# Output projections in products of 128 columns, four sums side by side in one PSUM bank

## The chip, the cores and the metric

The kernel runs on one core of one Trainium2 chip. The core has a matrix engine (TensorE, in the profile PE for matmuls and PEld for the loads of the stationary operand), a vector engine (DVE), a scalar engine (ACT), a general engine (POOL, or GpSimd) and a queue that issues most transfers (SP). Matmuls write into PSUM, eight banks of 2 KiB for each of 128 partitions; 512 float32 numbers fill one bank. The metric is the device time of one execution in microseconds (us).

## What is computed

One inference step of a decoder with two layers, for a prompt of 2048 tokens and for a sample batch of 8 sequences with 4 new tokens each (32 rows). Every layer normalises, projects in, mixes, projects out and adds the residual. The part that the change touches is the product with `w_out` at the end of either layer:

```python
def even_mixer(h, w_in, b_fox, lb, hgrn_gain, w_out, hgrn_s0, fox_attend):
...
    out = jnp.concatenate([o_a, o_b], axis=-1) @ w_out
    return out, s_a, kb_h, vb_h, log_fb

def odd_mixer(h, w_in, w_gate, b_gate, gla_gain, w_out, gla_s0):
...
    o = head_rmsnorm(o, gla_gain).reshape(bsz, L, C_VAL_WIDTH).astype(h.dtype) * jax.nn.silu(g)
    return o @ w_out, s

def run_trunk(...):
...
        x = x + out
    return rmsnorm(x, final_norm), ...
```

Here `w_out` is 1024 x 1024. The even layer has two groups of heads (a gated linear recurrence, and forgetting attention, which for the sample batch reads a paged cache of keys and values); the odd layer has one group, a gated linear recurrence.

## The kernel before

**Precision.** A float32 operand is held as two float16 parts, high and low, after scaling by a power of two. Every product is three matmuls into one sum: high by high, high by low, low by high (`mm3`, L476). Its three lines, L478 to L480, therefore stand for nearly all dense matmuls of the kernel, and groups of the profile are told apart by their tiles.

**Halves and units.** The 2048 prompt tokens are worked in two halves of 1024; the first half also carries the 32 sample rows. A half of a layer is a list of units, each with 256 (for one 272 or 260) columns of a weight. A unit has four stages: fetch the weights by DMA, measure their largest value, turn it into a scale, split into high and low parts (`half_unit`, L315; the split goes in four parts of two k-tiles each, L340). `staged` (L1070) runs these stages two to three units ahead of the matmuls.

**Output projections.** `out_units` (L1654) makes four units of 256 columns for each half and layer, with the weight's parts in the tile `w_o` and the sums in `pt_o`. They call `proj_tm` (L491), which puts tokens on the partitions: tokens come in tiles of 128 (`ttiles`, L391), two tiles make a pair, and a pair takes one PSUM bank (2 x 256 float32). For each of the two tiles, k runs over the eight k-tiles of 128 (KT), and each k is one `mm3` of 256 columns:

```python
            for j, (c0, n) in enumerate(grp):
                for k in range(KT):
                    self.mm3(ps[:n, j], [x[:, k, c0 : c0 + n] for x in act],
                             [x[:, k, :width] for x in W], k == 0, k == KT - 1)
```

The stationary operand is the activation tile, the moving one the weight. A pair is so 48 matmuls. Then `evac` (L1663) scales the sums and adds the residual: in layer 1 of the first half and layer 0 of the second through a tile `xo` that is loaded and stored by DMA, else in rows held on the chip (`row`). Three banks (tag "pj") rotate among all projections. In the last units of the kernel (second half, layer 1, u = 3) a pair is a single tile. The 32 sample rows go through `few_rows` (L510).

**Activations.** What is projected comes from DRAM: `y_pieces` (L1608) loads `yT` in pieces of 256 tokens and splits each, two k-tiles at a time, into high (ACT, L1632) and low parts (mostly DVE, L1633), into the tile `act`.

**Who else calls proj_tm.** The value projections of the recurrences (`Av`, `Cv`) and the keys and values of the attention (`Bk`, `Bv`).

**Order.** Generators for dense units and for the recurrences (`lin_attn`, L539) are woven by `mux` (L75) according to costs that they yield; `proj_tm` yields the same cost per pair before and after. The framework then plans each engine's instruction order with a clock of its own, so the order on an engine can differ from the program's. `issue_after` ties single instructions to others.

**Cache pages.** `fox_sample` (L1336) reads 128 pages of keys and then 128 of values, each 256 KB, into a ring of PG = 25 buffers (L1162); a load waits on SP until a buffer is free. On the same queue go the loads for the prompt's attention (`loads`, L1197), which runs in 16 groups beside it.

Of the kernel before, what the change touches and what calls it, by code (L numbers as in the profile page):

```python
# [11 lines left out]
F16 = mybir.dt.float16  # L12
# [7 lines left out]
P = 128  # L20
D = 1024
KT = D // P
# [23 lines left out]
PRT = ("st", "o")  # L46
REST_P = 18000.0
REST_S = 12200.0
PG = 25
PAST = 12  # L50
VAHEAD = 3
KAHEAD = 6
# [69 lines left out]
class Kern:  # L122
# [36 lines left out]
    def more_consts(self, mp):  # L159
        nc, i, cp, col = self.nc, self.i, self.cp, self.col  # L160
# [51 lines left out]
        self.mdiag = cp.tile([P, P], I8, name="mdiag")  # L212
        nc.vector.tensor_copy(self.mdiag, self.ident)

        self.bmask = cp.tile([P, DB, TS], F32, name="bmask")
        nc.gpsimd.memset(self.bmask, 1.0)
        nc.gpsimd.affine_select(self.bmask, self.bmask, [[-DS, DB], [1, TS]], ALU.is_ge, 0.0,
# [272 lines left out]

    def proj_tm(self, pps, act, W, hf, evac, nm, width=256, pairs=True):  # L491

        tl = self.ttiles(hf)
        per = 2 if width == 256 and pairs else 1
        for g in range(0, len(tl), per):
            grp = tl[g : g + per]
            n = grp[0][1]
            if n < P:
                evac(self.few_rows(pps, act, W, grp[0][0], nm, width), g, 1, n)
                yield 700  # L500
                continue
            ps = pps.tile([P, per, width], F32, tag="pj", name=f"pt_{nm}{g}")
            for j, (c0, n) in enumerate(grp):
                for k in range(KT):
                    self.mm3(ps[:n, j], [x[:, k, c0 : c0 + n] for x in act],
                             [x[:, k, :width] for x in W], k == 0, k == KT - 1)
            evac(ps[:n, : len(grp)], g, len(grp), n)
            yield 24 * len(grp) * 110

# [638 lines left out]
    def phase_fox(self):  # L1148
# [5 lines left out]
        if True:  # L1154
# [6 lines left out]
            with tc.tile_pool(name="fs", bufs=1, side="right", reuse_waits="tile") as s0:  # L1161
                fs = Pool(s0, {"pg": PG, "kt": 8})  # L1162
                self.prompt = self.fox_prompt(fx, pps, caus)
# [837 lines left out]
```

## Time and profile before

| | us |
|---|---|
| three runs | 2391.76, 2393.88, 2394.82 |
| median | 2393.88 |
| span of the profiled execution, first to last instruction | 2392.4 |
| PE busy in it | 2294.1 |

The profiled execution is one of its own; its span is compared with sums made from its rows, and the median with other kernels' runs. Views used below: the engine totals ("busy us (share of the span) xcount"); the chain of waits that ended last, by line; groups of instructions ("line engine op, out<-in, shapes xcount | busy, mean ns of one | idle time of the engine just before, and what ended it"); the order of time ("start, duration, engine, line, out<-in, xcount [idle before <-releaser]"); one tile's or line's instructions ("xcount: duration ns min/median/max, first and last start"); and stretches ("start:end length, PE busy (xcount), PEld, DVE, ACT, POOL, granted TensorE clock as a share of full, share of the DMA engines, GB/s"; asked of one tile, only the engines that work on it). A matmul's recorded end is modelled and overlaps the next start.

### The profile page before, as it was taken

The numbers are of one execution on the slowest core, as the hardware profiler recorded it, in microseconds if no ns is written. First come the engines' busy times: TensorE is split into PE (matmuls) and PEld (weight loads), VectorE is DVE, ScalarE is ACT, GpSimd is POOL, SyncE is SP. The second block draws the span as 40 slices with busy tenths as digits, with TensorE's granted clock in tenths as the row PEclk, the third lists the DMA queues.
The fourth block names the chain that finished last, engine by engine and source line by source line (L and its number), as shares of the span: only waits on it lengthen the run. The fifth ranks groups of instructions, "written<-read, shape, count | busy, mean of one in ns | idle before, by whom it ended". The sixth has DMA issues, their size and how long they took to land. (4 is left out here: it accounts for less than half of the span.)

```text
span 2392.4 us, 58667 instructions
## 1 busy us (share of the span) xinstructions
PE 2294.1 (96%) x23324; PEld 1633.7 (68%) x23324; DVE 1417.9 (59%) x3347; ACT 1107.5 (46%) x2458; POOL 753.7 (32%) x843
## 2 busy tenths in 40 slices
PE   6999999999999999999999999999999999999998
PEld 5677677864655875655446876777778766666887
DVE  7566556446655548666767463665675645557554
ACT  5334343342333226556667454535543635545333
POOL 2233222112212225234556211432452222322322
PEclk9999999999999999999999999999999999999999
DMA  6231234535541267676874632122156312114453
GB/s 198 63 88 58 81 113 142 175 92 143 149 136 43 85 192 258 223 251 203 270 241 134 213 109 58 46 81 86 50 151 196 111 41 70 43 59 159 154 192 147
DMA packets 297013, 317.24 MB, mean 133 GB/s; under 512 B 39730, under 2 KB 241011, under 8 KB 296739
## 3 DMA queue, kind: packets, MB, share of 16 engines
q1 hardware_dynamic: 295234, 308.98, 41.1%
q8 instruction: 183, 3.00, 0.5%
q0 software_dynamic: 1504, 4.52, 0.5%
q14 instruction: 92, 0.75, 0.1%
HBM read 242.31 MB, written 71.11 MB: 131 GB/s over the span
## 5 line engine op out<-in xcount | busy, mean ns | idle before, releaser
L480 PE MATMUL pt_o<-w_o,act 128*128 128x256 f16 x1024 | 280.5, 274 | 3.1 <-DVE act L1633 2.9
L478 PE MATMUL pt_o<-w_o,act 128*128 128x256 f16 x1024 | 280.7, 274 | 1.3 <-ACT sg1C L534 1.1
L479 PE MATMUL pt_o<-w_o,act 128*128 128x256 f16 x1024 | 280.5, 274 | 1.0 <-POOL w_o L353 1.0
L480 PEld LDWEIGHTS <-act 128*128 128x128 f16 x2304 | 226.6, 98 | 36.1 <-issue 4.6
L478 PEld LDWEIGHTS <-act 128*128 128x128 f16 x2304 | 226.6, 98 | 36.0 <-ACT act L473 4.0
L479 PEld LDWEIGHTS <-act 128*128 128x128 f16 x2304 | 226.7, 98 | 32.4 <-issue 2.9
L478 PE MATMUL pt_Cv<-w_Cv,act 128*128 128x256 f16 (+1 forms) x512 | 140.3, 275 | 1.7 <-ACT act L473 0.9
L644 POOL TENSOR_TENSOR kA<-kA,fA 128x512 f32<-128x512 f32 (+1 forms) x56 | 79.8, 1425 | 192.6 <-PE gl_A L610 143.0
L479 PE MATMUL pt_Cv<-w_Cv,act 128*128 128x256 f16 (+1 forms) x512 | 140.0, 274 | 0.0
L480 PE MATMUL pt_Cv<-w_Cv,act 128*128 128x256 f16 (+1 forms) x512 | 139.7, 274 | 0.0
L1241 ACT ACTIVATE L<-L,nm,kc 128x512 f32<-128x512 f32 (+3 forms) x160 | 118.2, 741 | 36.9 <-DVE nm L1239 27.2
L644 POOL TENSOR_TENSOR kC<-kC,fC 128x512 f32<-128x512 f32 (+1 forms) x56 | 81.8, 1461 | 148.2 <-PE gl_C L610 101.3
L1249 POOL TENSOR_SCALAR L<-L,nm 128x512 f32<-128x512 f32 (+3 forms) x160 | 98.8, 631 | 70.8 <-DVE nm L1245 28.6
L1276 ACT ACTIVATE th<-pt 128x512 f16<-128x512 f32 (+3 forms) x159 | 80.7, 527 | 59.8 <-PE pt L1269 58.9
L1277 DVE TENSOR_TENSOR tl<-pt,th 128x512 f16<-128x512 f32 (+3 forms) x159 | 94.4, 609 | 20.3 <-ACT th L1276 19.0
L1269 PE MATMUL pt<-ident,L 128*128 128x128 f32 x544 | 91.3, 280 | 4.9 <-DVE tl L1277 2.4
L1269 PEld LDWEIGHTS pt<-ident,L 128*128 128x128 f32 x544 | 66.7, 143 | 32.4 <-DVE tl L1277 9.1
L1393 PEld LDWEIGHTS pkt<-ident,pgcache_fox_k 128*128 128x128 f32 x512 | 58.1, 141 | 44.4 <-issue 25.6
L1393 PE MATMUL pkt<-ident,pgcache_fox_k 128*128 128x128 f32 x512 | 76.1, 279 | 4.7 <-DVE kts L1397 2.0
L478 PE MATMUL pt_Av<-w_Ai,act 128*128 128x256 f16 x256 | 70.9, 277 | 1.9 <-ACT act L473 1.9
L479 PE MATMUL pt_Av<-w_Ai,act 128*128 128x256 f16 x256 | 70.7, 276 | 0.4 <-DVE w_Ai L346 0.4
L478 PE MATMUL pt_Bk<-w_Bk,act 128*128 128x256 f16 x256 | 71.0, 277 | 0.0
(952 smaller groups left out, 6738.3 us busy)
## 6 DMA issues: line engine op xcount, KB each, us to landing
pgcache_fox_k<-in_cache_fox_k SPq DMA_DIRECT2D x128, 256.0 KB, 4.2
pgcache_fox_v<-in_cache_fox_v SPq DMA_DIRECT2D x128, 256.0 KB, 4.2
yr<-yT SPq DMA_DIRECT2D x16, 1024.0 KB, 7.4
nx<-in_x_prompt SPq DMA_DIRECT2D x16, 512.0 KB, 5.4
wr_Aqf<-in_w_in_even SPq DMA_DIRECT2D x64, 128.0 KB, 3.2
wr_o<-in_w_out_even SPq DMA_DIRECT2D x32, 256.0 KB, 4.5
wr_Cv<-in_w_in_odd SPq DMA_DIRECT2D x32, 256.0 KB, 3.8
wr_Cqk<-in_w_in_odd SPq DMA_DIRECT2D x64, 128.0 KB, 2.8
```

Of the source, the lines that this page charges most:

```text
L478: nc.tensor.matmul(ps, lh[0], rh[0], start=first, stop=False)
L479: nc.tensor.matmul(ps, lh[0], rh[1], start=False, stop=False)
L480: return nc.tensor.matmul(ps, lh[1], rh[0], start=False, stop=last)
L644: nc.gpsimd.tensor_tensor(kv[:, :, 0], kv[:, :, 0], t1.to_broadcast([P, nb, w]), ALU.mult)
L1241: self.last_exp = nc.scalar.activation(lt[:, :w], lt[:, :w], AF.Exp, bias=nm[:, 0:1], scale=ib, accum_out=nm[:, 2 + j : 3 + j])
L1249: nc.gpsimd.tensor_scalar(lt[:, :w], lt[:, :w], nm[:, 1:2], 2.0**14, ALU.mult, ALU.mult)
L1269: nc.tensor.transpose(pt[:, w : w + P], rows[b][s // 4][0][:, (s % 4) * P : (s % 4 + 1) * P], self.ident)
L1276: nc.scalar.activation(th[:, a:w], pt[:, a:w], AF.Copy),
L1277: nc.vector.tensor_tensor(tl[:, a:w], pt[:, a:w], th[:, a:w], ALU.subtract)))
L1393: nc.tensor.transpose(pk[:, j * P : (j + 1) * P], pgs[j][:, h * P : (h + 1) * P], self.ident)
```

## The change

```diff
-PG = 25
+PG = 24
...
+        self.zero = cp.tile([P, P], F16, name="zero")
+        nc.gpsimd.memset(self.zero, 0.0)
...
-        tl = self.ttiles(hf)
+        nc, tl = self.nc, self.ttiles(hf)
...
             ps = pps.tile([P, per, width], F32, tag="pj", name=f"pt_{nm}{g}")
-            for j, (c0, n) in enumerate(grp):
+            if nm[0] == "o":
                 for k in range(KT):
-                    self.mm3(ps[:n, j], [x[:, k, c0 : c0 + n] for x in act],
-                             [x[:, k, :width] for x in W], k == 0, k == KT - 1)
+                    for j, (c0, n) in enumerate(grp):
+                        for h in (0, P):
+                            self.mm3(ps[:n, j, h : h + P], [x[:, k, c0 : c0 + n] for x in act],
+                                     [x[:, k, h : h + P] for x in W], k + j + h == 0, (k, j, h) == (KT - 1, len(grp) - 1, P))
+            else:
+                for j, (c0, n) in enumerate(grp):
+                    for k in range(KT):
+                        self.mm3(ps[:n, j], [x[:, k, c0 : c0 + n] for x in act],
+                                 [x[:, k, :width] for x in W], k == 0, k == KT - 1)
```

Only the output projections change (their names begin with "o"). Each product of 256 columns becomes two of 128, so a pair is 96 matmuls, each with its own load of the stationary operand. The loop over k moves outside the loop over the two tiles, and so four sums, two tiles by two column halves, grow side by side in the bank. Only the first matmul of the bank has the start flag and only the last the stop flag. A tile of 128 x 128 float16 zeros is added, which no instruction reads, and the ring of cache pages has one buffer less.

## The prediction

> **What bounds the kernel now.** I read the page from its engine totals, then the chain of waits, then the groups of the output projections, then the order of time inside them.
>
> ```profile
> span 2392.4 us, 58667 instructions
> PE 2294.1 (96%) x23324; PEld 1633.7 (68%) x23324; DVE 1417.9 (59%) x3347; ACT 1107.5 (46%) x2458; POOL 753.7 (32%) x843
> PE pt_o L479 3%; PE pt_o L478 3%; PE pt_o L480 3%; PE pt_Cv L478 2%; PE pt_Cv L479 2%; PE pt_Cv L480 2%; DMA yr<-yT 2%; PE o_C L764 1%; PE gl_C L610 1%; DVE qC L643 1%; DMA wr_Cv<-in_w_in_odd 1%; DMA x1d<-row 1%; DVE scT L625 1%; DVE act L1633 1%; PE py_C L582 0%
> L480 PE MATMUL pt_o<-w_o,act 128*128 128x256 f16 x1024 | 280.5, 274 | 3.1 <-DVE act L1633 2.9
> L478 PE MATMUL pt_o<-w_o,act 128*128 128x256 f16 x1024 | 280.7, 274 | 1.3 <-ACT sg1C L534 1.1
> L479 PE MATMUL pt_o<-w_o,act 128*128 128x256 f16 x1024 | 280.5, 274 | 1.0 <-POOL w_o L353 1.0
> ```
>
> TensorE is busy for 96% of the span, and the three lines of mm3 that write `pt_o` head the chain. So a microsecond added to a dense stretch of these products is a microsecond of the kernel, unless PE was about to wait there anyway. There are 3 x 1024 = 3072 products. Their waits are few: 3.1 + 1.3 + 1.0 = 5.4 us in all. The mean of 274 ns is not the price, because matmuls overlap; the price is the step from one start to the next.
>
> ```profile
> 2299.84 0.27 PE L480 MATMUL pt_o<-w_o,act 128*128 128x256 f16 x1
> ...
> 2302.89 0.27 PE L478 MATMUL pt_o<-w_o,act 128*128 128x256 f16 x1
> 1904.83 0.38 PE L479 MATMUL pf_C10q<-act,w_Cqk 128*128 128x512 f16 x1
> ...
> 1908.29 0.38 PE L480 MATMUL pf_C10q<-act,w_Cqk 128*128 128x512 f16 x1
> ```
>
> Between the first two rows lie 28 steps: 3.05 / 28 = 0.1089 us for 256 columns. Between the other two lie 16 steps: 3.46 / 16 = 0.2163 us for 512. A column therefore costs (0.2163 - 0.1089) / 256 = 0.42 ns, and about 1.5 to 2.5 ns per matmul is left that does not shrink with the columns.
>
> **The change part by part.** *Two products of 128 for one of 256.* 3072 matmuls with their weight loads become 6144. By the straight line, 128 columns step in 0.1089 - 128 x 0.00042 = 0.0552 us. The trace also has such matmuls, in trains of three:
>
> ```profile
> L479 PE MATMUL fo<-tl,h_v x174: 219/379/634, 897.0 to 1310.2; 128*128 128x512 f16 x99, 128*128 128x256 f16 x43, 128*128 128x128 f16 x17, 128*128 128x384 f16 x15
> ...
> 969.22 0.22 PE L478 MATMUL fo<-th,h_v 128*128 128x128 f16 x1
> 969.28 0.22 PE L479 MATMUL fo<-tl,h_v 128*128 128x128 f16 x1
> 969.33 0.22 PE L480 MATMUL fo<-th,l_v 128*128 128x128 f16 x1
> 969.39 0.39 PE L1269 MATMUL pt<-ident,L 128*128 128x128 f32 x2
> 969.22 0.10 PEld L479 LDWEIGHTS <-h_v 128*128 128x128 f16 x1
> 969.28 0.10 PEld L480 LDWEIGHTS <-l_v 128*128 128x128 f16 x1
> ```
>
> Three steps take 0.17 us, 0.0567 each, and the weight loads start 0.06 apart as well: every matmul has its own full load and does not wait for it. I take 0.0556, between the line and this train. A product then costs 2 x 0.0556 - 0.1089 = 0.0023 us more, and 3072 of them **+7.1 us** (the two ends, 0.0552 and 0.0567, give +4.6 and +13.8). All of it lies on PE.
>
> *The weight loads.* 3072 more of them. Whether a long stream of 128-column matmuls is held up by them is the point on which most depends.
>
> ```profile
> L480 PEld LDWEIGHTS <-act 128*128 128x128 f16 x2304 | 226.6, 98 | 36.1 <-issue 4.6 <-DVE act L1633 4.1
> ...
> 1235.88 0.10 PEld L478 LDWEIGHTS <-h_v 128*128 128x128 f16 x1 [0.85 <-issue]
> 1235.90 0.10 PEld L478 LDWEIGHTS <-h_q 128*128 128x128 f16 x1
> 785.70:807.90 22.20, 22.20 (x519) 19.23 (x518) 13.74 (x30) 3.69 (x9) 8.24 (x7) 1.00 0.15 51
> ```
>
> A row of a load lasts 98 ns. If that were its hold on the array, 6144 x 0.098 = 602 us would stand in place of 335. But after an idle stretch two loads start 0.02 us apart, so 98 ns is a latency. The last row, a stretch of busy times by engine, shows the supply of instructions: 519 matmuls and 518 loads in 22.2 us, 21 ns an instruction without idle time; the new stream needs one per 28 ns. So I cost the loads at nothing beyond the step above, and keep 602 - 335 = +267 us as the far bound, since no train of the trace is longer than three.
>
> [...]
>
> *The order of the steps.* With k outermost, both token tiles of a pair use an eighth of the weights or activations before the next is asked for. Where these arrive late, PE now has twice the work to put in front of each arrival.
>
> ```profile
> 1335.32 0.27 PE L479 MATMUL pt_o<-w_o,act 128*128 128x256 f16 x1 [0.75 <-POOL w_o L353]
> 2303.33 0.27 PE L479 MATMUL pt_o<-w_o,act 128*128 128x256 f16 x1
> 2304.98 0.28 PE L480 MATMUL pt_o<-w_o,act 128*128 128x256 f16 x1 [1.38 <-DVE act L1633]
> 2307.38 0.39 PE L480 MATMUL pt_o<-w_o,act 128*128 128x256 f16 x1 [1.57 <-DVE act L1633]
> 2304.19 0.73 DVE L1633 SCALAR_TENSOR_TENSOR act<-yr,kc,act 128x512 f16<-128x512 f32 x1
> 2306.57 0.75 DVE L1633 SCALAR_TENSOR_TENSOR act<-yr,kc,act 128x512 f16<-128x512 f32 x1
> 2308.14 5.00 DVE L1633 SCALAR_TENSOR_TENSOR act<-yr,kc,act 128x512 f16<-128x512 f32 x6
> 2300.00:2308.30 8.30, 5.35 (x45) 0.88 (x2) 0.90 0.86 284
> 2308.30:2314.00 5.70, 5.59 (x30) 0.86 (x2) 0.55 0.41 131
> ```
>
> At 1335.32 the first pair of a unit waits for the third quarter of its weights, k = 4. That quarter would now be asked for after 24 products instead of 12, 1.3 us later: the wait goes, **-0.9 us** (0.75 idle and the 0.27 - 0.11 by which the matmul before it seems to last on). At 2303 the first pair after a reload waits for the low halves of its activations, which DVE delivers at 2304.92, 2307.32, 2308.87 and then every 0.72. The first wait stays. After 2304.98 PE would work 1.3 us, wait until 2307.4, and then hardly wait. At full clock the pair would end near 2311.6. Now it ends near 2314.8: some 4 of the 40 products left at 2307.38 start by 2308.3, by the last row 30 take the next 5.7 us, because the granted clock is down there (0.55), and the last 6 take 0.109 each. A mean of 0.55 is half clock until 2313.4. If it stays so, the new order ends near 2314.4. So the gain is 0.4 to 3.2 us. The row nearest to it is the clock that was granted, so I take **-0.4**. [...]
>
> That pair waits for data, so the products just ahead of it (the row below, 2278 to 2303) may each be 2.3 ns longer for nothing, **-0.5 us**.
>
> ```profile
> 2278.00:2303.00 25.00, 23.29 (x208) 2.24 (x3) 1.00 0.73 241
> ```
>
> *Evacuation, stores, queues.* Each pair still ends in one bank with the same evacuation; no DMA, semaphore or queue position is moved. Three such banks rotate, so 10.5 us of matmuls cover an evacuation. Without the cover the rows show 1.1 us, once (L478 above). Zero.
>
> *One page buffer fewer, and a tile of zeros.* Nothing reads the zeros; their store is one memset on POOL, at the start.
>
> ```profile
> 0.81 0.20 POOL masks.py:197 MEMSET ident<- 128x128 f32 x1 [0.29 <-POOLq L1989]
> L1393 PE MATMUL pkt<-ident,pgcache_fox_k x512: 272/273/475, 901.3 to 1100.6; 128*128 128x128 f32 x171
> L1363 SPq DMA_DIRECT2D pgcache_fox_k<-in_cache_fox_k x128: 327/333/1977, 890.4 to 1064.9; - x128
> L1363 SPq DMA_DIRECT2D pgcache_fox_v<-in_cache_fox_v x128: 332/333/1857, 1065.5 to 1243.4; - x128
> DMA to landing us min/median/max: 2.5/4.2/6.5
> SPq L1363 <- PE pkt L1393: 51.4, 47, 6.0
> ```
>
> The memset costs 0 to 0.2 us by the row for the identity; I take 0. Loads of cache pages do wait on SP for a free buffer (47 waits, 51.4 us). With 24 buffers each load goes out up to one page later, (1064.9 - 890.4) / 127 = 1.37 us. The last page is issued 1100.6 - 1064.9 = 35.7 us before its last transposition and lands in 4.2, so pages stay early. Behind a waiting page load on SP stand the loads of the next prompt group (L1197 to L1204), issued after the first block of a group and first split after its third; a group, 440 us / 16 = 27 us by the stretch shown below, leaves them a cover of some 13 us. Zero; without that cover, 1.37 us for each of the 353 / 27 = 13 groups of the paged stretch, +18 us.
>
> **Sum:** 7.1 - 0.9 - 0.4 - 0.5 = **+5.3 us** on the profiled 2392.4, that is 2397.7. The median of the runs shown, 2393.88, lies 1.5 us above the profiled span, so the forecast is 2393.9 + 5.3 = **2399.2 us**. The least change that a measurement of this kernel can tell is about 0.2%, 4.8 us; the forecast is just past it.
>
> **The rivals.** *The order gives the cost back (not slower).* Place: the pair at 2303 and the weights at 1335. If the clock is not taken down, 3.2 + 0.9 + 0.5 us return, and 2396.4 remains. For it: the second wait shrinks from 1.57 + 0.27 to about 1 us. Against it: the first wait of 1.65 us stays. It decides from the point where that pair ends before 2314.
>
> *The stream is bound by its weight loads.* Up to +267 us, 2661, by the 98 ns rows, or anything from a step above 57 ns on. For it: only trains of three are shown. Against it: the loads 0.02 us apart. [...]
>
> *Another order on the engines.* The planner sets each engine's order from its own clock, and 3072 more matmuls and a shorter page ring shift that clock. The stretches with idle time on PE are these (stretch, its length, PE busy):
>
> ```profile
> 870.00:1310.00 440.00, 412.67 (x2903) 244.51 (x2901) 304.79 (x939) 277.66 (x625) 215.56 (x325) 0.97 0.70 228
> 1390.00:1757.00 367.00, 351.52 (x3870) 260.81 (x3869) 213.01 (x451) 188.84 (x409) 113.21 (x98) 1.00 0.23 74
> 2302.80:2314.80 12.00, 8.95 (x54) 6.13 (x52) 9.72 (x15) 4.71 (x14) 3.78 (x4) 0.72 0.54 173
> ```
>
> 27.3 + 15.5 + 3.1 = 45.9 us idle. An order that adds a third of this gives 2414 (with the page ring's +18, up to 2417); one that takes a third away gives 2384. Nothing in the trace says which.
>
> **How the numbers follow.** Forecast 0.43; cost given back 0.26; another order, worse 0.14, better 0.12; bound by loads 0.05. Slower is the first, the worse order and the last: 0.62. Same is the second: 0.26; the edges that the first two cases have beyond the 4.8 us are set against each other. Faster is the better order: 0.12. The range runs from 2388 to 2413: it holds the first two cases and most of the worse and part of the better order, and leaves out the far ends and the load bound, under 0.2 together. The likeliest case alone spans 2396.7 to 2405.9, by the steps of 0.0552 and 0.0567.
>
> **What would show it.** In the changed profile the rows of `pt_o` should number 6144, of 128 columns, with starts 0.055 to 0.056 apart inside a pair, over dozens in a row. [...] The four stretches of output projections should each be about 1.8 us longer, and the wait at about 1335 gone; at about 2303 the second wait should be under 1.2 us, and the granted clock decides between the forecast and its first rival. Page loads should wait on SP a little longer and PE no more between 870 and 1310. The prediction is wrong if PE idles there by more than 5 us otherwise than before, or if the step is not near 0.056.

## The result, and the profile after

The changed kernel takes 2407.11 us (median of four runs, 2405.00 to 2409.14); the kernel before took 2392.9 us (median of four) on the same chip. The ratio is 1.0058, with a 95% interval from 1.0042 to 1.0075: between 10 and 18 us slower. The forecast had the sign, and 5.3 of the 14 us.

First the page of the changed kernel: the span, the engine totals and the groups of the output projections (lines stand two to nine further down than before).

```profile
span 2405.9 us, 64805 instructions
PE 2298.2 (96%) x26396; PEld 1679.8 (70%) x26396; DVE 1415.5 (59%) x3347; ACT 1107.4 (46%) x2458; POOL 754.5 (31%) x844
L480 PE MATMUL pt_o<-w_o,act 128*128 128x128 f16 x2048 | 350.7, 220 | 2.3 <-DVE xo L1679 1.5
L482 PE MATMUL pt_o<-w_o,act 128*128 128x128 f16 x2048 | 350.3, 220 | 2.4 <-DVE act L1642 2.4
L481 PE MATMUL pt_o<-w_o,act 128*128 128x128 f16 x2048 | 350.3, 220 | 0.4 <-POOL w_o L355 0.4
```

There are 3 x 2048 = 6144 matmuls of 128 columns, as announced. PE is busy 4.1 us more (2298.2 against 2294.1), but the span grew by 13.5: some 9 us are new idle time of PE. (The busy time also holds the drops of the clock. The trace before has 67.9 us at half clock, a drop of 10.2 us at 364 among them, which is missing here, and the trace of the changed kernel has 54.6; so 4.1 is less than the change itself added.) The waits in front of the products themselves did not grow (5.1 us here, 5.4 before). So two questions: what is a step of the new stream, and where does PE stand idle?

The step, from the order of time in the last output projection:

```profile
2329.82 0.22 PE L481 MATMUL pt_o<-w_o,act 128*128 128x128 f16 x1
...
2333.23 0.22 PE L482 MATMUL pt_o<-w_o,act 128*128 128x128 f16 x1
```

Between these rows lie 61 steps: 3.41 / 61 = 0.0559 us. Over all dense gaps of the trace the mean is 55.83 ns, against 109.16 for 256 columns before. A product costs 2 x 55.83 - 109.16 = 2.5 ns more, and 3072 of them 7.7 us.

The rest is found by following single instructions through both traces and subtracting their starts. Three stretches differ most. The first is that of the cache's value pages; the windows from 1130 to 1190 of the kernel before and of the changed one (length, then busy time of PE, PEld, DVE, ACT and POOL, granted clock, DMA share, GB/s):

```profile
1130.00:1190.00 60.00, 56.59 (x367) 29.01 (x366) 45.31 (x151) 40.72 (x96) 33.35 (x51) 1.00 0.84 276
```
```profile
1130.00:1190.00 60.00, 52.47 (x329) 26.76 (x327) 39.67 (x129) 36.87 (x87) 31.24 (x47) 0.97 0.86 282
```

PE does 38 matmuls less in the same 60 us, and idles 7.5 us instead of 3.4. The order of time in the changed kernel shows the place:

```profile
1147.34 1.91 PE L1541 MATMUL pv<-pgcache_fox_v,pT 128*16 128x512 f32 x16
1151.79 1.78 PE L1541 MATMUL pv<-pgcache_fox_v,pT 128*16 128x512 f32 x8 [2.54 <-DMA pgcache_fox_v<-in_cache_fox_v]
```

PE has the probabilities and waits 2.54 us for values. It takes the pages in fours, and the wait ends with the landing of the last of the four, the 56th page, at 1151.55. The same products before the change, in one piece:

```profile
1151.08 2.77 PE L1532 MATMUL pv<-pgcache_fox_v,pT 128*16 128x512 f32 x24
```

The second and third stretch lie where an output projection is woven with a recurrence. Rows of the changed kernel, with PE's waits:

```profile
1870.57 0.44 PE L442 MATMUL nt<-ident,x1r 128*128 128x128 f32 x2 [2.43 <-DVE y_C L602]
```
```profile
2198.08 0.22 PE L480 MATMUL pt_o<-w_o,act 128*128 128x128 f16 x1 [0.84 <-ACT sg1C L543]
2200.84 0.72 PE L619 MATMUL gl_C<-qC,kC 128*31 128x16 f32 x64 [1.09 <-DVE qC L573]
2209.77 0.88 PE L619 MATMUL gl_C<-qC,kC 128*30 128x16 f32 x64 [2.58 <-DVE qC L652]
2216.58 0.71 PE L619 MATMUL gl_C<-qC,kC 128*28 128x16 f32 x64 [0.76 <-DVE qC L652]
```

At 1870 PE stands 2.43 us for an instruction on DVE (`y_C`) that it did not wait for before. In exchange its waits for `qC` earlier in the same stretch shrank, from 3.7 us in three places to 1.75 in one. In the third stretch it waits 5.3 us in four places, where the kernel before waited 3.1 us in two:

```profile
2191.66 0.27 PE L478 MATMUL pt_o<-w_o,act 128*128 128x256 f16 x1 [1.13 <-ACT sg1C L534]
2204.38 0.72 PE L610 MATMUL gl_C<-qC,kC 128*30 128x16 f32 x64 [1.96 <-DVE sam_o L517]
```

The order on PE differs there. Counted in products of 256 columns, the recurrence's diagonal product `gd_C` stood behind 39 output products before and stands behind 21.5 now; its first levels `gl_C` behind 86, 138 and 172 before, and 61.5, 111 and 144 now.

**Theory A**, for the experiments: three costs add up, each with its own cause: the longer step (7.7 us), the ring with one page less, and the planner's other order; the reordering of k gives a few us back. **Rivals**: the ring costs nothing and what is seen in its stretch is chance; the order costs nothing and its stretches are only longer by the steps; the stream is held by its weight loads, so that another width would show it.

### The profile page after: what moved, and what is told of

Same layout as the page of the kernel before. It is cut to its first block, busy times and chain, and to the rows that moved or that the text cites. A ratio compares the mean times of both kernels' runs of the same rounds, so it can differ in the third digit from the quotient of the medians.

```text
span 2405.9 us, 64805 instructions
## 1 busy us (share of the span) xinstructions
PE 2298.2 (96%) x26396; PEld 1679.8 (70%) x26396; DVE 1415.5 (59%) x3347; ACT 1107.4 (46%) x2458; POOL 754.5 (31%) x844
## 3 DMA queue, kind: packets, MB, share of 16 engines
q8 instruction: 207, 3.39, 0.6%
## 5 line engine op out<-in xcount | busy, mean ns | idle before, releaser
L480 PE MATMUL pt_o<-w_o,act 128*128 128x128 f16 x2048 | 350.7, 220 | 2.3 <-DVE xo L1679 1.5
L482 PE MATMUL pt_o<-w_o,act 128*128 128x128 f16 x2048 | 350.3, 220 | 2.4 <-DVE act L1642 2.4
L481 PE MATMUL pt_o<-w_o,act 128*128 128x128 f16 x2048 | 350.3, 220 | 0.4 <-POOL w_o L355 0.4
L480 PEld LDWEIGHTS <-act 128*128 128x128 f16 x3328 | 327.4, 98 | 25.0 <-ACT act L475 4.1
L482 PEld LDWEIGHTS <-act 128*128 128x128 f16 x3328 | 327.4, 98 | 21.3 <-issue 2.8
L481 PEld LDWEIGHTS <-act 128*128 128x128 f16 x3328 | 327.6, 98 | 20.4 <-issue 2.6
L480 PE MATMUL pt_Av<-w_Ai,act 128*128 128x256 f16 x256 | 71.2, 278 | 2.8 <-ACT act L475 2.8
L481 PE MATMUL pt_Av<-w_Ai,act 128*128 128x256 f16 x256 | 70.9, 277 | 0.4 <-DVE w_Ai L348 0.4
L482 PE MATMUL pt_Av<-w_Ai,act 128*128 128x256 f16 x256 | 71.0, 278 | 0.0
```

The source lines that it names most:

```text
L480: nc.tensor.matmul(ps, lh[0], rh[0], start=first, stop=False)
L481: nc.tensor.matmul(ps, lh[0], rh[1], start=False, stop=False)
L482: return nc.tensor.matmul(ps, lh[1], rh[0], start=False, stop=last)
```

## The experiments

The kernel before ran beside each group of experiments: 2394.86 us (median) beside e1 to e4, 2394.17 beside e5 to e8, 2394.26 beside e9 and e10. Differences in us are (ratio - 1) x 2394.

**e1: the change without the shorter ring and the zeros.**

```diff
-PG = 24
+PG = 25
...
-        self.zero = cp.tile([P, P], F16, name="zero")
-        nc.gpsimd.memset(self.zero, 0.0)
```
(against the changed kernel)

> The change without the tile of zeros and with the ring of 25 cache pages. Theory A (three terms: matmul steps of 55.8 ns make the products 2 x 55.8 - 109.2 = 2.5 ns dearer, 7.7 us; the shorter ring costs 3 to 6 us between 1120 and 1190; the rest is another order around the projections): 6 to 11 us over the kernel before, and no wait of a value product for a cache page at about 1150. Rival B (all of the 14 us is the split): 13 to 15 us over. Rival C (the step alone decides, ring and order are chance): 7 to 8 us over.

Measured: 2405.34 us (6 runs), ratio 1.0042, 1.0026 to 1.0059: 10 us slower than before, 6 to 14. Most of the cost stays without the shorter ring, so the ring is not the whole of it; whether it is the missing 4 us can't be read from intervals so wide, and e2 asks it directly.

**e2: the shorter ring alone.**

```diff
-PG = 25
+PG = 24
```

> The kernel before with a ring of 24 cache pages and nothing else. Theory A: 3 to 6 us over the kernel before, PE idle for a cache page once at about 1150 and the TensorE clock taken down behind it. Rivals B and C, and the prediction's own term: 0, within 1 us.

Measured: 2400.11 us (12 runs), ratio 1.0022, 1.0010 to 1.0034: 5.3 us. Most of the difference between the two traces (6.5 of 7.4 us) arises among the value pages, with the same row as in the changed kernel. The order of time, then the window:

```profile
1156.67 1.80 PE L1532 MATMUL pv<-pgcache_fox_v,pT 128*16 128x512 f32 x8 [2.52 <-DMA pgcache_fox_v<-in_cache_fox_v]
```
```profile
1130.00:1190.00 60.00, 54.07 (x338) 27.19 (x338) 40.82 (x141) 36.55 (x86) 28.97 (x45) 0.97 0.86 282
```

No product was split here, and the wait of 2.5 us stands at the same four pages. It is the ring's. Over the whole stretch PE idles 5.3 us more; what the wait for the pages does not explain of it lies in later waits, mostly for DVE.

**e3 and e10: k outermost, 256 columns, ring of 25** (the same kernel twice).

```diff
+            if nm[0] == "o":
                 for k in range(KT):
-                    self.mm3(ps[:n, j], [x[:, k, c0 : c0 + n] for x in act],
-                             [x[:, k, :width] for x in W], k == 0, k == KT - 1)
+                    for j, (c0, n) in enumerate(grp):
+                        self.mm3(ps[:n, j], [x[:, k, c0 : c0 + n] for x in act],
+                                 [x[:, k, :width] for x in W], k + j == 0, (k, j) == (KT - 1, len(grp) - 1))
```
(against the kernel before; other projections stay as they are)

> The kernel before with k outermost in the output projections and products of 256 columns as before. Theory A: 1 to 4 us under the kernel before (the wait for weights at 1335 gone, the wait for activations at 2303 shorter). Rival D (the order of the steps is worth nothing, since another wait ends last there): within 1 us.

> The kernel of e3 once more, unchanged, as the one that e9 stands against and to see whether it is ahead of the kernel before a second time. Theory A (the reordering of k alone saves what the prediction counted for it, 0.9 + 0.4 to 3.2 + 0.5 us): 1.8 to 4.6 us under the kernel before. Rival (e3 was chance): within 1 us of it.

Measured: 2391.43 us, ratio 0.9984 (0.9973 to 0.9995), and 2392.12 us, ratio 0.9991 (0.9978 to 1.0004), 12 runs each: 3.8 and 2.2 us faster. One interval leaves out "no change", the other just holds it. The order of time in e10 at the pair that waits for its reloaded activations, and the window around it:

```profile
2307.08 0.28 PE L480 MATMUL pt_o<-w_o,act 128*128 128x256 f16 x1 [1.78 <-DVE act L1639]
2309.48 0.28 PE L480 MATMUL pt_o<-w_o,act 128*128 128x256 f16 x1 [0.92 <-DVE act L1639]
```
```profile
2300.00:2314.00 14.00, 11.22 (x100) 9.34 (x98) 8.59 (x14) 5.92 (x12) 2.52 (x3) 1.00 0.80 269
```

The first wait stays, the second shrinks to 0.92 us, and the granted clock is 1.00: the 192 products of this unit (the first of the second half's layer 1) take 3.1 us less than before. In e3, with a drop of 3.4 us there, they take 1.9 us less. It is what the first rival of the prediction described, in a kernel without the split. Its medians are the lowest of all. It is clearly ahead of the changed kernel, and ahead of the kernel before by one of the two intervals.

**e4: 128 columns, but k inside, as before the change.**

```diff
-                for k in range(KT):
-                    for j, (c0, n) in enumerate(grp):
+                for j, (c0, n) in enumerate(grp):
+                    for k in range(KT):
                         for h in (0, P):
```
(against e1, with the flags for each tile)

> Products of 128 columns with the two tiles of a pair one after the other as before, ring of 25. Theory A: 1 to 3 us over the first kernel of this call, so 8 to 13 over the kernel before. Rival D: the same as the first kernel of this call.

Measured: 2406.07 us (7 runs), ratio 1.0034, 1.0017 to 1.0052: 8 us slower than before, 4 to 12. The split alone costs about what e1 costs. That k outermost gives some us back, as between e3 and the kernel before, is not seen between e1 and e4: their intervals overlap, and the difference has the other sign. Their traces do differ as expected at the last reload (the 192 products of that unit take 2.4 us less than before in e1, the same as before in e4).

**e5: four products of 64 columns.**

```diff
-                        for h in (0, P):
+                        for h in (0, 64, 128, 192):
-                            self.mm3(ps[:n, j, h : h + P], [x[:, k, c0 : c0 + n] for x in act],
-                                     [x[:, k, h : h + P] for x in W], k + j + h == 0, (k, j, h) == (KT - 1, len(grp) - 1, P))
+                            self.mm3(ps[:n, j, h : h + 64], [x[:, k, c0 : c0 + n] for x in act],
+                                     [x[:, k, h : h + 64] for x in W], k + j + h == 0, (k, j, h) == (KT - 1, len(grp) - 1, 192))
```
(against e1)

> Four products of 64 columns for one of 256, ring of 25 pages, k outermost, no tile of zeros. Theory A (every matmul adds a fixed 2.4 ns or so to its columns at 0.42 ns each): a step of 26.7 + 2.4 = 29 ns, so a product of 256 columns takes 4 x 29 - 109 = 7 ns more, 3072 of them 22 us; with the other order of the engines on top (2 to 5 us) +22 to +28 us on the kernel before, about 2416 to 2422 us. Rival (a matmul with its own weight load can't start less than about 55 ns after the one before it): 4 x 55 - 109 = 111 ns a product, +340 us.

Measured: 2459.67 us (5 runs), ratio 1.0270, 1.0252 to 1.0287: 65 us. The rival falls, but theory A's sum misses too. Groups of the page, then the order of time:

```profile
span 2455.0 us, 77106 instructions
L478 PE MATMUL pt_o<-w_o,act 128*128 128x64 f16 x4096 | 379.0, 195 | 14.1 <-issue 13.7
L480 PE MATMUL pt_o<-w_o,act 128*128 128x64 f16 x4096 | 378.8, 195 | 12.8 <-issue 12.5
L479 PE MATMUL pt_o<-w_o,act 128*128 128x64 f16 x4096 | 378.7, 195 | 7.3 <-issue 6.8
```
```profile
1311.57 0.19 PE L478 MATMUL pt_o<-w_o,act 128*128 128x64 f16 x1
...
1313.88 0.19 PE L479 MATMUL pt_o<-w_o,act 128*128 128x64 f16 x1
...
1330.93 0.19 PE L479 MATMUL pt_o<-w_o,act 128*128 128x64 f16 x1 [3.42 <-issue]
```

Between the first two rows lie 79 steps: 2.31 / 79 = 29.2 ns, just as theory A had it. Over all dense gaps the mean is 29.16: 4 x 29.16 - 109.16 = 7.5 ns a product, 23 us. The other cost is new: 33.0 us in which PE waits "for issue", that is for nothing that the profile shows. The last section comes back to it. What remains of the 65 us, some 9, is mostly clock: 409 steps of 53 or 54 ns, at half clock, cost 10 us over steps of 29, where the kernel before has 24 steps of 213 ns instead of 109, 2.5 us. In the changed kernel no product waits for issue.

**e6 and e7: the change in one half of the units each**, ring of 25: e6 in the units that run dense (o00 and o11), e7 in those woven with a recurrence (o01 and o10).

```diff
-            if nm[0] == "o":
+            if nm[:3] in ("o00", "o11"):
```
(against e1; in e7 `("o01", "o10")`)

> The change in half of the output projections only (the units o00 and o11, which are not woven with the memory layers), ring of 25. Theory A (the step): 1536 products x 2.5 ns = +3.8 us, with few rows of the engines' order changed: +2 to +6 us. Rival (the order sets it, not the step): within 1.5 us of the kernel before, or over +8.

> The change in the other half only (o01 and o10, woven with the memory layers' work), ring of 25. Theory A: +3.8 us for the step, and on top the two re-ordered stretches (about 1843 to 1900 and 2184 to 2226, +3.0 and +4.4 us in the changed kernel): +5 to +11 us, with these stretches longer in its trace too. Rival (those stretches were chance of the clock): +3 to +5 us and no longer stretches.

Measured: e6 2397.47 us (12 runs), ratio 1.0008, 0.9997 to 1.0020; e7 2400.81 us (11 runs), ratio 1.0021, 1.0010 to 1.0031: 1.9 and 5.0 us. The number of split products is the same, 1536, so the 3.1 us between them (the intervals overlap from 1.0010 to 1.0020) are not the step. But they are not the order of the engines alone: e6 also holds the two places at which the order of k was to gain, 1335 and 2303, and e7 neither. By time e7 lies where theory A and its rival meet, so the traces have to decide. The order on PE went with the split: e1, e4 and e7 have `gd_C` and `gl_C` in the last recurrence behind just as many products as the changed kernel, e3, e6 and e10 behind as many as the kernel before. The rows of e7 that answer to those of the changed kernel:

```profile
1871.58 0.44 PE L440 MATMUL nt<-ident,x1r 128*128 128x128 f32 x2 [1.61 <-DVE y_C L600]
```
```profile
PE gl_C L617 <- DVE qC L571: 3.1, 2, 2.0
PE gl_C L617 <- DVE qC L650: 3.1, 2, 2.6
```

(The second fence is the table of PE's waits over the whole trace: total, times, longest.) In e6 the wait for `y_C` is not there (in e10, with no product split, it is 0.67 us), and the waits for `qC` are 1.1 and 2.5 us, the longest 1.8. By starts of the same instructions, in us against the kernel before:

| stretch | length before | changed | e1 | e2 | e6 | e7 | e9 | e10 |
|---|---|---|---|---|---|---|---|---|
| value pages, 1132.7 to 1227.4 | 94.7 | +6.1 | 0.0 | +6.5 | +2.4 | 0.0 | +2.1 | -0.1 |
| o01 and norms, 1752.0 to 1900.6 | 148.6 | +2.7 | +2.7 | +0.8 | +0.2 | +3.5 | +0.6 | +1.2 |
| o10 and last recurrence, 2181.3 to 2225.7 | 44.4 | +4.5 | +4.0 | -0.3 | -0.1 | +3.9 | +3.9 | +2.0 |

The value pages cost only where the ring is shorter (e6 and e9 each have 3.4 us more at half clock there than the kernel before). In the woven stretches of the split kernels the steps explain 1.9 us of the second row and 0.7 of the third. The lengths also hold drops of the clock: 3.4 us at half clock, worth 1.7 us, in the second row of e7 and in the third row of the changed kernel, e1, e7 and e10. And a column is one execution: the profiled one of e1 took 2398.38 us, 7 us under the median, that of e7 2405.24, 4.4 over. PE's idle time in the same two stretches is free of the steps; in us against the kernel before:

| stretch | idle before | changed | e1 | e4 | e7 | e9 | e3 | e6 | e10 |
|---|---|---|---|---|---|---|---|---|---|
| o01 and norms | 4.4 | +1.0 | +0.9 | +1.1 | +0.2 | +0.1 | +0.7 | -0.3 | +0.5 |
| o10 and last recurrence | 3.2 | +2.2 | +1.6 | +3.4 | +1.3 | +3.8 | +0.1 | -0.1 | +0.4 |

In the last recurrence the kernels with the other order (the changed one, e1, e4, e7, e9) idle 1.3 to 3.8 us more (most in e4 and e9, where no drop of the clock slows PE), those with the order of before 0.4 us or less: there the order costs. In o01 the split kernels (0.2 to 1.1 us) can't be told from the others (-0.3 to 0.7), so a cost of the order isn't shown there.

**e8: a ring of 23 pages, nothing else.**

```diff
-PG = 25
+PG = 23
```

> The kernel before with 23 page buffers and nothing else changed. Theory A (each buffer fewer shortens the lead of the value pages on their use, which is down to 6.3 us with 25): more and longer waits of the products of values for their pages, between the 65th and the 193rd, +6 to +14 us. Rival (what 24 buffers cost was an accident of its order): 0 to +5 us and no more waits for value pages than with 24.

Measured: 2401.12 us (12 runs), ratio 1.0025, 1.0012 to 1.0038: 6 us, at the lower edge of theory A and hardly more than with 24. The table of PE's waits of e8:

```profile
PE pv L1532 <- DMA pgcache_fox_v<-in_cache_fox_v: 2.2, 2, 1.2
```

Two waits of 1.2 us or less in place of one of 2.5. So the cost does not rise evenly with every buffer; theory A was too simple in that. That it also matters where the loads of the prompt's attention fall among the pages on SP is a guess, and wasn't tested.

**e9: the order alone.** The kernel of e3, with PE's order in the last recurrence tied to that of the changed kernel.

```diff
+        i = self.count = getattr(self, "count", -1) + 1
+        n = sum(i >= x for x in (22, 62, 111, 144, 192, 208, 240, 288))
+        return self.tc.issue_after(self.lv[min(n, len(self.lv)) - 1].ins) if n else ExitStack()
```
(for each product of o10; `self.lv` holds the last matmul of gd_C and of each gl_C)

> 256 columns, k outermost, ring of 25 as in e3, but PE's order in the last woven recurrence is tied to that of the changed kernel: the first diagonal product gd_C after 22 output products of 256 columns instead of 39, the seven levels gl_C after 62, 111, 144, 192, 208, 240 and 288 instead of 86, 138, 172, 192, 223, 253 and 288. No matmul is split. Theory A (the planner's other order is a cost of its own): PE waits for q and k of the recurrence as in the changed kernel, and the stretch from 2184 to 2226 is 2 to 4 us longer than in e3; the kernel 2 to 4 us over e3. Rival (that stretch is longer only because its matmuls are split): no longer than in e3, within 1 us.

Measured: 2394.30 us (12 runs), ratio 1.0005, 0.9991 to 1.0019: 3 us over e10, with intervals that overlap. The stretch itself is clearer; windows of e9, then of e10, then of the kernel before:

```profile
2180.30:2228.60 48.30, 41.27 (x761) 34.28 (x759) 37.36 (x68) 17.35 (x36) 13.88 (x11) 1.00 0.58 184
```
```profile
2181.00:2227.40 46.40, 42.75 (x761) 35.21 (x759) 37.08 (x68) 16.41 (x32) 14.43 (x11) 0.96 0.58 187
```
```profile
2181.30:2225.70 44.40, 41.18 (x761) 34.33 (x759) 37.07 (x68) 16.41 (x32) 14.43 (x11) 1.00 0.63 195
```

The same 761 matmuls; PE idles 48.30 - 41.27 = 7.0 us in e9, 3.7 in e10 and 3.2 before. So the order costs 3.4 to 3.8 us of idle time here, with no matmul split. (The stretch of e10 is only 1.9 us shorter than that of e9, because e10 has a drop of the clock in it that e9 lacks.) The long waits stand before the same products as in the changed kernel, the second and third level of `gl_C` (here `sam_o` ends the latter, there `qC`):

```profile
2202.00 0.72 PE L626 MATMUL gl_C<-qC,kC 128*30 128x16 f32 x64 [2.96 <-DVE qC L660]
2208.67 0.71 PE L626 MATMUL gl_C<-qC,kC 128*28 128x16 f32 x64 [2.24 <-DVE sam_o L532]
```

The reverse, the split with the order of before, wasn't tried.

## Why the prediction was right and wrong

**The sum as measured:** step 7.7; ring 5.3 (e2, 2.4 to 8.1); the other order 1.3 to 3.8 (new idle time in the last recurrence; by time e9 is 3 us over e10, with intervals that overlap); k outermost 1.1 to 4 given back (1.1 in the trace of the changed kernel, see the third and fourth point below; 2 to 4 in e3 and e10). That makes 10 to 16 us against 14 measured (10 to 18): the sum closes, but it is too wide to settle its two smaller terms. One comparison stays open: e1 differs from e3 by the split alone, and is 14 us slower (2405.34 against 2391.43, both beside the same runs of the kernel before), where step and order come to 9 to 11.5. With e1's six runs this may be noise, or k outermost gains less once the products are split. The prediction had 7.1, 0, 0 and -1.8.

The time, 2407.1, lies inside the range that was stated, and slower came. The forecast's own sum did not bring it there, and the likeliest case ended at 2405.9. The range held because it left room for another order on the engines; the ring's 5.3 us, put at nothing, came on top. That the time still fell inside is luck in part.

- **The step** (2.3 ns a product, +7.1): right. Measured 2.5 ns, 7.7 us, between the two ends given. The straight line had given 55.2 ns and the train of three 56.7; the long streams step in 55.8.
- **The load rival**: fell. Loads run under the matmuls at 55.8 ns, and at 29.2 in e5. (The trace of before did hold one train of four, at 1243.91, with steps of 0.057 us as well.) The long streams keep a straight line: (109.16 - 55.83) / 128 = 0.4166 ns a column between 128 and 256 columns, which leaves 55.83 - 128 x 0.4166 = 2.5 ns a matmul; for 64 columns it gives 29.2 ns, and e5 measured 29.16.
- **The wait at 1335** (-0.9): right. The wait for the third quarter of the weights is gone. The one that is left, 0.37 us, is another: it stands at the second product of the unit, for the first quarter, and the kernel before has it too, with 0.28. Together PE waits 0.7 us less here. With k inside (e4) the wait for the third quarter is back. Rows of the kernel before, the changed kernel and e4:

```profile
1333.10 0.27 PE L479 MATMUL pt_o<-w_o,act 128*128 128x256 f16 x1 [0.28 <-POOL w_o L353]
```
```profile
1335.45 0.22 PE L481 MATMUL pt_o<-w_o,act 128*128 128x128 f16 x1 [0.37 <-POOL w_o L355]
```
```profile
1338.47 0.22 PE L479 MATMUL pt_o<-w_o,act 128*128 128x128 f16 x1 [0.73 <-POOL w_o L353]
```

- **The pair at 2303** (-0.4, or 3.2 if the clock stays): both ends came. In the changed kernel the stretch of 192 products grew by 0.1 us, 0.5 of steps and -0.4 of the rest; in e10, at full clock, it shrank by 3.1. (The -0.5 us of steps hidden in front of the wait can't be told apart in it.) But the path to the -0.4 differs from the one described, and that the number fits is luck. A wait of 1.47 for `xo` came in ahead. The second wait should have been under 1.2 us and is 1.94: on DVE the sample rows' `xo` now stands between the two deliveries and waits there 2.32 us for its own DMA (the fourth row); before, it stood ahead of both. And the drop of the clock came later and shorter (the last row, a window; it was 6.8 us long before).

```profile
2312.45 0.22 PE L480 MATMUL pt_o<-w_o,act 128*128 128x128 f16 x1 [1.47 <-DVE xo L1679]
2318.59 0.23 PE L482 MATMUL pt_o<-w_o,act 128*128 128x128 f16 x1 [0.50 <-DVE act L1642]
2322.04 0.23 PE L482 MATMUL pt_o<-w_o,act 128*128 128x128 f16 x1 [1.94 <-DVE act L1642]
2320.85 0.47 DVE L1679 SCALAR_TENSOR_TENSOR xo<-few_o,kc,xo 32x256 f32<-32x256 f32 x1 [2.32 <-DMA xo<-x1d]
```
```profile
2322.70:2326.10 3.40, 3.40 (x36) 3.40 (x34) 3.37 (x7) 1.94 (x4) 0.93 (x1) 0.51 0.29 95
```

- **The ring** (zero): wrong, and the step that failed is its cover. It was read from the end of the key pages, where a load goes out 35.7 us before its use. The 128 value pages run through the same ring, and there the lead had to be taken page by page. Counted in the trace of before, from a load's issue to the first product with its page, it falls from 50.9 us at the first page to 5.0 at the 28th, and to 5.0 again at the 56th. Both of these landed after 4.0 us (the median of all is 4.2, the longest 6.6). So the cover was not some 31 us, as at the end of the key pages, but 1 us at the tightest. With 24 buffers the lead of the pages from the 29th to the 52nd is 0.3 to 4.2 us shorter, and PE is ready for the next four, from the 53rd to the 56th, 1.8 us after the load of the last has gone out. The rows of SP, before and after the change, show it from the other side (start, duration of the issues, number):

```profile
1142.93 0.90 SPq L1363 DMA_DIRECT2D pgcache_fox_v<-in_cache_fox_v  x2
1143.93 0.38 SPq L1169 DMA_DIRECT2D raw_v<-vd  x1
1146.53 10.49 SPq L1363 DMA_DIRECT2D pgcache_fox_v<-in_cache_fox_v  x12
```
```profile
1140.39 0.38 SPq L1178 DMA_DIRECT2D raw_v<-vd  x1
1141.51 14.78 SPq L1372 DMA_DIRECT2D pgcache_fox_v<-in_cache_fox_v  x16
```

Before, the first of the 12 pages went out at 1146.5 and was used at 1152.8. After, the same page goes out at 1145.8, as the fifth of 16 behind the prompt's loads, and PE is at it at 1149.25. The far end that the prediction kept, +18, was never near: the wait comes once, not in each of 13 groups.

- **Another order on the engines** (a rival, 0.14 for worse): this came, but beside the forecast, not in its place. The forecast counted it at zero since nothing in the trace gives its size. It was to be had in part: the place where it is shown, the last recurrence, is one where split units are woven with a recurrence, and PE waited there already (`gl_C` for DVE, 1.96 us). The bound for PE's idle time between 870 and 1310, 5 us, held by a little: the same stretch of the changed kernel (window below) has 445.4 - 413.6 = 31.8 us instead of 27.3. That PE would idle no more there did not come true; 4.1 of these 4.5 us lie among the value pages and are the ring's, which the bound was not meant for.

```profile
866.80:1312.20 445.40, 413.58 (x2904) 244.51 (x2902) 304.37 (x939) 277.51 (x625) 215.54 (x325) 0.97 0.70 225
```

## What to carry to other kernels

A ring of buffers is judged where its lead is shortest, not at its end: list issue and use of every load, and compare the least lead with the longest landing. Each product that was split cost 2.5 ns more here, although its loads stayed hidden at steps of 55.8 ns, and the split also moved the planner's clock, so wherever the split work is woven with something that waits, the order has to be looked at again. A change made of several parts is worth taking apart: here the part that gains (k outermost, 2 to 4 us by itself) was covered by those that lose.

## What the hardware showed that was not expected

**The supply of instructions.** The prediction took 21 ns an instruction as enough for the new stream, and it was: no product of the changed kernel waited for issue. In e5 the stream asks for one per 14.6 ns (a load and a matmul in 29.2), and PE stood still for 33.0 us in 20 waits for issue on `pt_o`. The lines of the DMA queue marked "instruction" (packets, MB, share), of the kernel before, of the changed kernel and of e5:

```profile
q8 instruction: 183, 3.00, 0.5%
```
```profile
q8 instruction: 207, 3.39, 0.6%
```
```profile
q8 instruction: 255, 4.18, 0.7%
```

From the changed kernel to e5 these are 48 packets more for 77106 - 64805 = 12301 instructions more, and from the kernel before to the changed one 24 for 64805 - 58667 = 6138: 256 instructions for a packet both times, and 3.39 MB / 207 = 16 KB a packet. An estimate by these counts: a packet holds 128 loads and 128 matmuls, and they last 128 x 29.2 ns = 3.7 us in e5 and 128 x 55.8 ns = 7.1 us in the changed kernel. In e5's trace each of the 20 waits ends 2.2 to 3.0 us after a packet of queue 8 starts, though the 255 packets are 9.6 us apart in the mean (2455.0 / 255). That what PE waits for is its instructions is the author's reading of these numbers; no run tested it. In a window of e5 around the wait at 1330.93 the DMA engines are full (share 1.01):

```profile
1327.30:1331.00 3.70, 0.28 (x11) 0.19 (x8) 2.55 (x6) 3.70 (x9) 2.41 (x4) 1.00 1.01 373
```

That the packet came late there behind other transfers is a guess. It would not be the whole: the stretch from 2225 to 2265 holds waits of 2.50 and 3.52 us, and its share is 0.48 in the mean. In seven of the waits (17 us together) the share of the DMA engines is over 0.9, but in eight (7 us, one of them 2.30 us long) it is under 0.3. What sets these waits was not tested.

**The granted clock.** In e3 and e10 the same kernel has its drops of the granted clock at other places (3.4 us at 2311.0 in e3, none there in e10). In all 66.2 us of e3's trace are at half clock and 55.9 of e10's, and e3's span is 4.2 us longer. A single trace's stretch is therefore compared by PE's idle time, not by its length, where a drop falls into one of the two.
